# A three-branch decoder layer on one core: mLSTM, then cross-attention, then differential attention, with the output projection in two parts

## The chip, the cores and the metric

The kernel runs on one core of one Trainium2 chip. The metric is device time in microseconds (us) of one execution; of several executions of one program the median is taken. TensorE (PE in the profile) multiplies matrices, VectorE (DVE), ScalarE (ACT) and GpSimd (POOL) work on vectors, and SyncE (SP) only issues transfers (DMA) between device memory (DRAM) and the core's own memory. Each engine runs its instructions in the order in which they stand.

## What is computed

The layer normalises x (1024 tokens x 1024), projects it by one matrix of 9 groups of 512 columns, lets three groups of four heads work on the result, gates each, and maps the 1536 columns back onto the residual stream. All is float32.

```
h = rmsnorm(x, norm_g)
x_m, o_m, z_m, q_d, k_d, v_d, z_d, q_c, z_c = split(h @ w_in)         # 9 x 512
# mLSTM: q, k of silu(conv(x_m)), v of x_m; gates of (q, k, v); 8 chunks of 128 tokens,
# each with the state C, n of the chunk before it
y_m = (head_layernorm(sigmoid(o_m) * mlstm(q, k, v, gates)) + skip * x_cv) * silu(z_m)
# differential attention: two causal softmax maps a head (64 wide each), one less lam times the other
y_d = rmsnorm((softmax(q0 k0) - lam * softmax(q1 k1)) @ v_d) * silu(z_d)
# cross-attention on 256 rows of mem
y_c = softmax(q_c k_m) @ v_m * silu(z_c)
out = rmsnorm(x + concat(y_m, y_d, y_c) @ w_out, final_g)
```

## The kernel before

**Tiles.** Tokens lie in 8 row blocks of 128. Each large product is made of operands that are split in a high and a low part, so that a product over 128 rows of the inner dimension is three matmuls (high-high, high-low, low-high); a projection of 128 columns for 512 tokens is 8 x 3 = 24 matmuls of 128x512. `load_w` loads a weight block of 512 KB ahead of its use, in the order in which `plan_w` lists them, and splits it on POOL and DVE.

**What sets the order.** The code is written in one order, and a scheduler then places each engine's instructions in a fixed order of its own, so that work of several stages stands mixed. Buffers come from pools (`BUFS`): 16 "h" buffers hold the normalised and transposed x (`hT`), 8 "w" the split weights, 12 "qk", 5 "g" (halves, for gates), 4 "vd", 4 "p", 2 "pT", 2 "od"; a tile waits until the one that had its buffer is done. In PSUM, where matmuls write, there are two buffers each of three kinds.

**The order in the code.** (1) The norm and transposes of mem, `km_head`, the eight `x_block`, `vm_cols`, the cross heads (`cross_weights`, `cross_proj`, `cross_core`). (2) `vd_cols`, then four heads of differential attention: `diff_proj(h)` makes q and k; `diff_block(h, j)` treats the 128 queries of row block j against (j+1) blocks of 128 keys: scores of two maps (`ds`, L417, L418, L420), a row maximum on DVE (L421), exponentials on ACT (L424), a scaling on POOL (L428), the difference on DVE (L430), transposes on PE (`dpt`, L437), copies on ACT and DVE (L441, L439), the product with v (`dov`, L444) and its copy (L445). The j of a head run 0, 7, 1, 6, 2, 5, 3, 4. `diff_z` makes the gate, `diff_finish` norms and stores a head's rows to the DRAM tensor Yd. (3) The mLSTM: `xm_proj`, `om_cols`, `kv_block`, `qk_head`, gates, and then `chunk(c)` and `chunk_out(c)`. (4) The output: `load_wo` loads w_out (12 transfers of 512 KB), `out_prefetch(c)` reads rows back from Yd, and `out_block(c)` multiplies all 12 blocks of 128 columns by w_out, adds x, norms and stores.

Stages 3 and 4 are interleaved: the gate product `zm` (`zm_half`) stands among the first chunks, and out_block(c) stands beside chunk(c+2) and chunk_out(c+1). A chunk reads back from DRAM what stage 3 wrote there: k and v (`kvc`), q and k (`t`), a row of gate numbers broadcast to all 128 partitions (`rbc`, twice 256 KB), and, in chunk_out, two gates (`soz`) and the skip term (`skc`): 2.25 MB a chunk.

The loop that mixes the last two stages:

```
    for c in range(NB):
        if 0 < c and c + 2 < NB:
            chunk(c + 2)
        if 0 < c < NB - 1:
            chunk_out(c + 1)
        if 1 < c + 1 < NB:
            out_prefetch(c + 1)
        out_block(c)
```

Of the kernel before, what the change touches and what calls it, by code (L numbers as in the profile page):

```python
# [32 lines left out]
def hybrid_layer(ctx: ExitStack, tc: tile.TileContext, x, mem, norm_g, w_in, conv_w, conv_b, wq_m, wk_m,  # L33
# [76 lines left out]
    for cg in range(2):  # L110
        plan_w(w_in, C_VD + 256 * cg, f"wvd{cg}", True)
    for h in range(H):
        for c0, n_, hh in ((C_QD, "wqd", h), (C_KD, "wkd", h), (C_ZD, "wzd", h - 1)):
            if hh >= 0:
                plan_w(w_in, c0 + hh * P, f"{n_}{hh}")
    plan_w(w_in, C_OM, "wom0", True)
    plan_w(w_in, C_ZD + 3 * P, "wzd3")
    for h in range(H):
        plan_w(w_in, C_XM + h * P, f"wxm{h}")
    plan_w(w_in, C_OM + 256, "wom1", True)  # L120
    for h in range(H):
# [49 lines left out]
    def norm_transpose(src, blocks, g_, tag, sink):  # L171
        gbc, gsrc = g_
        for b in blocks:
# [16 lines left out]
    mT = [[slot("vd", f"mT{g}{part}", F32R).rearrange("p (k m) -> p k m", k=4) for part in range(2)]  # L190
          for g in range(2)]
# [142 lines left out]
    split_w(vmh, vml, vm, pool)
    mn = cst.tile([P, H], F32, name="mn")
    sk = cst.tile([P, H], F32, name="sk")
    cb = cst.tile([P, H], F32, name="cb")
    cw = cst.tile([P, 4, H], F32, name="cw")
    bif = cst.tile([P, 8], F32, name="bif")
    load(out=mn, in_=mnorm_g[0].rearrange("(h p) -> p h", p=P))  # L340
    load(out=sk, in_=skip_m[0].rearrange("(h p) -> p h", p=P))
    load(out=cb, in_=conv_b[0].rearrange("(h p) -> p h", p=P))
    for k in range(4):
        load(out=cw[:, k, :], in_=conv_w[0][k].rearrange("(h p) -> p h", p=P))
# [549 lines left out]
```

## Time and profile before

| | us |
|---|---|
| median of 3 runs | 817.94 (817.21 to 820.07) |
| the profiled execution | 819.47 |
| its span, from the first instruction to the last | 817.7 |
| TensorE busy | 770.1 |

The page has a line for each engine with its busy time, and the span in slices; the same table can be had for stretches that one chooses, with the clock that TensorE was granted (1.00 is 2.4 GHz, 0.50 is 1.2 GHz) and the share of time in which the 16 DMA engines were busy. In the order of time the span holds: the start and the cross heads (0 to 240 us), differential attention with products of the mLSTM among it (240 to 545), the rest of the mLSTM's preparation (545 to 605), the chunks with the output projection (605 to 745), and the rest of the output projection. Lists of waits say for how long an engine stood idle ahead of a kind of instruction, and which instruction released it; the timeline gives single instructions with the idle time before them in brackets.

### The profile page before, as it was taken

Reading aid. Unit: us, or ns where it says so; the run is one execution under the profiler, and the core shown is the slowest. Engines: PE = TensorE matmul, PEld = TensorE weight load, DVE = VectorE, ACT = ScalarE, POOL = GpSimd, SP = SyncE. Lnnn points to the kernel's source line nnn. Section 1 sums busy time; section 2 is a strip of 40 time slices with the busy share of each in tenths; the row PEclk is TensorE's granted clock in tenths of the full one; section 3 lists DMA queues with packets and bytes.
Section 4 is the critical chain, followed back from the end, with each engine's and each line's share of the span. In section 5 each row is a group of like instructions: output and inputs, shape, how many; then the busy total and the mean of one; then the engine's idle time right before and its main releaser. Section 6 shows DMA issues by size and latency. Waiting matters only on the chain.

```text
span 817.7 us, 11784 instructions
## 1 busy us (share of the span) xinstructions
PE 770.1 (94%) x4432; PEld 663.9 (81%) x4432; DVE 445.2 (54%) x922; ACT 322.3 (39%) x753; POOL 192.6 (24%) x248
## 2 busy tenths in 40 slices
PE   4999999999999999989999999999786879989996
PEld 3988888899988888878898888998565768777886
DVE  5785244342257667667724578533633597556532
ACT  3435234331134455545554437544472342222211
POOL 5443113121111122313103312412132332212000
PEclk9999999999999999999999999999898999999999
DMA  9920312122110001100122020245897997763001
GB/s 254 316 83 15 89 53 78 31 61 78 52 52 27 26 28 51 52 26 25 54 72 71 27 78 26 61 172 181 258 314 205 299 270 248 220 185 115 26 26 52
DMA packets 106416, 89.09 MB, mean 109 GB/s; under 512 B 10480, under 2 KB 91376, under 8 KB 106360
## 3 DMA queue, kind: packets, MB, share of 16 engines
q1 hardware_dynamic: 106216, 88.08, 35.7%
q8 instruction: 35, 0.57, 0.3%
q10 hardware_dynamic: 144, 0.26, 0.1%
q14 instruction: 21, 0.17, 0.1%
HBM read 65.23 MB, written 23.10 MB: 108 GB/s over the span
## 4 chain that ended last, share of the span: by engine, by line
PE 76%; DMA 11%; DVE 4%; issue 3%; POOL 2%; SPq 2%; ACT 2%; POOLq 0%; DVEq 0%; ACTq 0%
PE op L806 8%; PE om L158 6%; PE zd L149 5%; PE kd L149 5%; PE xm L149 5%; PE qd L149 5%; DMA rbc<-RBd 5%; PE qc L149 5%; PE zc L149 5%; PE vd L158 5%; PE zm L149 4%; PE dov L444 4%; PE ds L417 2%; PE ds L418 2%; PE dpt L437 2%
## 5 line engine op out<-in xcount | busy, mean ns | idle before, releaser
L806 PE MATMUL op<-wo,yh 128*128 128x512 f32 (+1 forms) x272 | 84.1, 391 | 2.4 <-DVE szm L667 2.4
L424 ACT ACTIVATE dp<-ds,dnb 128x128 f32<-128x128 f32 (+7 forms) x64 | 47.2, 740 | 55.3 <-DVE dnb L422 52.2
L149 PE MATMUL zm<-hT,wzm 128*128 128x512 f32 x192 | 51.0, 421 | 11.0 <-DVE szm L667 8.1
L806 PEld LDWEIGHTS op<-wo,yh 128*128 128x128 f32 x272 | 50.6, 193 | 12.5 <-DVE szm L667 2.8
L428 POOL TENSOR_SCALAR dp<-dp,dsum 128x128 f32<-128x128 f32 (+7 forms) x32 | 27.0, 844 | 135.8 <-DVE dsum L427 90.6
L421 DVE TENSOR_REDUCE dnb<-ds 128x1 f32<-128x128 f32 (+7 forms) x64 | 47.3, 752 | 19.9 <-PE ds L420 19.7
L149 PEld LDWEIGHTS zm<-hT,wzm 128*128 128x128 f32 x192 | 38.6, 205 | 20.4 <-DVE szm L667 8.7
L806 PE MATMUL op<-wo,yl 128*128 128x512 f32 (+1 forms) x136 | 52.6, 387 | 0.0
L158 PE MATMUL om<-wom,hT 128*128 128x256 f32 x384 | 52.4, 287 | 0.0
L149 PE MATMUL kd<-hT,wkd 128*128 128x512 f32 x192 | 49.6, 402 | 0.0
L149 PE MATMUL xm<-hT,wxm 128*128 128x512 f32 x192 | 48.7, 400 | 0.0
L149 PE MATMUL zd<-hT,wzd 128*128 128x512 f32 x192 | 48.7, 400 | 0.0
L149 PE MATMUL qd<-hT,wqd 128*128 128x512 f32 x192 | 48.3, 399 | 0.0
L806 PE MATMUL op<-wo,ymr 128*128 128x512 f32 (+1 forms) x204 | 47.8, 382 | 0.1
L158 PEld LDWEIGHTS om<-wom,hT 128*128 128x128 f32 x384 | 47.4, 189 | 0.1
L149 PE MATMUL qc<-hT,wqc 128*128 128x512 f32 x192 | 47.2, 394 | 0.0
L149 PE MATMUL zc<-hT,wzc 128*128 128x512 f32 x192 | 46.8, 393 | 0.0
L158 PE MATMUL vd<-wvd,hT 128*128 128x256 f32 x384 | 46.2, 279 | 0.0
L158 PEld LDWEIGHTS vd<-wvd,hT 128*128 128x128 f32 x384 | 45.1, 188 | 0.3
L806 PEld LDWEIGHTS op<-wo,ymr 128*128 128x128 f32 x204 | 36.5, 188 | 8.2 <-DVE ymr L84 0.5
L149 PEld LDWEIGHTS qc<-hT,wqc 128*128 128x128 f32 x192 | 35.5, 188 | 7.3
L149 PEld LDWEIGHTS zc<-hT,wzc 128*128 128x128 f32 x192 | 35.5, 188 | 7.3
(331 smaller groups left out, 1658.3 us busy)
## 6 DMA issues: line engine op xcount, KB each, us to landing
wor<-in_w_out_dram SPq DMA_DIRECT2D x12, 512.0 KB, 6.1
xx<-in_x_dram SPq DMA_DIRECT2D x8, 512.0 KB, 5.8
KVd<-kv SPq DMA_DIRECT2D x8, 512.0 KB, 2.7
QKd<-qkt SPq DMA_DIRECT2D x16, 256.0 KB, 3.6
kvc<-KVd SPq DMA_DIRECT2D x16, 256.0 KB, 7.1
yr<-Yd SPq DMA_DIRECT2D x8, 512.0 KB, 10.0
t<-QKd SPq DMA_DIRECT2D x8, 512.0 KB, 7.1
rbc<-RBd SPq DMA_DIRECT2D x16, 256.0 KB, 9.6
```

Of the source, the lines that this page charges most:

```text
L149: pe.matmul(acc, lhsT=w[wp][:, k, :], rhs=hT_ap(t, k, hp, 0, 512), start=n == 0, stop=n == 23)
L158: pe.matmul(acc, lhsT=hT_ap(b // 4, k, hp, (b % 4) * P, P), rhs=w2[k // 4][wp][:, k % 4, :], start=n == 0, stop=n == 23)
L417: pe.matmul(sc[:, c0:c0 + w_], lhsT=lhs, rhs=KA[h][m][:, c0:c0 + w_], start=True, stop=False)
L418: pe.matmul(sc[:, c0:c0 + w_], lhsT=lhs, rhs=KB[h][m][:, c0:c0 + w_], start=False, stop=not last)
L421: dve.tensor_reduce(out=nb[:, m:m + 1], in_=sc[:, :n], op=ALU.max, axis=AX.X)
L424: act.activation(p_[:, :n], sc[:, :n], AF.Exp, scale=0.125, bias=nb[:, m:m + 1], accum_out=sums[:, m:m + 1])
L428: pool.tensor_scalar(out=pp[1][:, :n], in0=pp[1][:, :n], scalar1=sums[:, 1:2], scalar2=0.0, op0=ALU.mult, op1=ALU.add)
L437: pe.transpose(out=pt[:, i * P:(i + 1) * P], in_=pp[0][:, (g + i) * P:(g + i + 1) * P], identity=ident)
L444: pe.matmul(acc, lhsT=pT[:, i * P:(i + 1) * P], rhs=vd[h][:, i, :], start=i == 0, stop=i == j)
L806: pe.matmul(accs[nh][:, c0:c0 + n_], lhsT=yp[a_], rhs=wo[kp, nh, b_][:, o:o + n_], start=k == 2 * KORD[0] and n == 0, stop=k == 2 * KORD[- ...
```

## The change

The arithmetic is the same but for the order of sums. The order of the stages is turned round:

- The start: pairs of `x_block`, and after each pair `xm_pair(h, g)` for the four heads, that is xm for 256 tokens by matmuls of 256 columns (384 in all in place of 192 of 512). 6 of the 8 normed rows come from "qk" buffers, and the low parts of wxm0 and wxm1 are made on POOL.
- The mLSTM's preparation follows (conv, kv_block, qk_head, gates, both om_cols), then the chunks, with `zm_head`, the norm of mem, `km_head`, `vm_cols` and `vd_cols` among them. chunk_out no longer splits its rows for the output projection, but stores them to Yd (8 stores of 256 KB), which has 12 column blocks now: 0 to 3 mLSTM, 4 to 7 cross, 8 to 11 differential.
- Then the cross heads, then the four heads of differential attention. Loads of w_out stand after head 2: into "h" buffers, which the last uses of hT have let go, and for two of six pairs of blocks into "w" buffers.
- The output projection is cut in two. `out_part(c)` multiplies the mLSTM and cross columns (48 matmuls a row block) and adds x; `out_final(c)` multiplies the differential columns (24), adds, norms and stores. out_part's rows (`yr`) take an "od" buffer. The order is out_part(0) to (3), diff_finish(3), out_part(4) to (7), out_final(0) to (7). The last row block's two halves are scaled by DVE one after the other; before, ACT and DVE did one half each.

```diff
-    for h in range(H):
-        for i, j in enumerate((0, 7, 1, 6, 2, 5, 3, 4)):
-            diff_block(h, j)
-            if h and i == 2:
-                diff_finish(h - 1)
-        if h + 1 < H:
-            diff_proj(h + 1)
-        diff_z(h)
-        if h == 2:
-            om_cols(0)
...
-        ymr = ymr_[c] = slot("pT", f"ymr{c}", F32R)
-        split(ymr[:, :512], ymr[:, 512:], ym)
+        store(out=Y[c][:, 0:4, :].rearrange("p k s -> p (k s)"), in_=ym)
...
+    def out_part(c):
+        xr = XR[c] = slot("qk", f"xr{c}")
+        load(out=xr, in_=x[c * P:(c + 1) * P, :])
+        yr = slot("od", f"yr{c}")
+        load(out=yr, in_=Y[c][:, 0:8, :].rearrange("p k s -> p (k s)"))
+        yp = [slot("qk", f"yp{c}{i}", F32R) for i in range(2)]
+        split(yp[0], yp[1], yr)
         for nh in range(2):
+            acc = pj(f"oa{c}{nh}")
+            products(acc, yp, (0, 1, 4, 5), nh)
             cs = slice(nh * 512, (nh + 1) * 512)
             dve.tensor_tensor(out=xr[:, cs], in0=acc, in1=xr[:, cs], op=ALU.add)
...
+    for g in range(4):
+        x_block(2 * g)
+        x_block(2 * g + 1)
+        for h in range(H):
+            xm_pair(h, g)
...
+    om_cols(0)
+    om_cols(1)
     chunk(0)
     chunk(1)
+    for h in range(H):
+        zm_head(h)
...
     chunk_out(0)
...
     chunk(2)
+    km_head(0)
+    km_head(1)
     chunk_out(1)
+    km_head(2)
+    chunk(3)
+    km_head(3)
+    chunk_out(2)
+    vm_cols(0)
+    chunk(4)
+    vm_cols(1)
...
+    diff_proj(0)
+    for h in range(H):
+        for i, j in enumerate((0, 7, 1, 6, 2, 5, 3, 4)):
+            diff_block(h, j)
+            if h and i == 2:
+                diff_finish(h - 1)
+        if h < H - 1:
+            diff_proj(h + 1)
+        if h < H - 2:
+            diff_z(h)
+        if h == H - 2:
+            for kps, t in (((0, 1), 0), ((4, 5), 1)):
+                diff_z(h, (t,))
+                diff_z(h + 1, (t,))
+                for kp in kps:
+                    load_wo(kp, "w", "h")
+    for kp in (2, 3):
+        load_wo(kp, "p", "w")
+    for c in range(4):
+        out_part(c)
+    diff_finish(H - 1)
+    FG.append(slot("p", "fg"))
+    load(out=FG[0], in_=final_g.partition_broadcast(P))
+    for c in range(4, NB):
+        out_part(c)
     for c in range(NB):
+        out_final(c)
```

Three places of the order that the scheduler made follow; a name such as ds361 is the scores of head 3, row block 6, map 1, and the number behind the underscore is that of a buffer.

TensorE in head 3 of differential attention, before: the scores of (3,6), then what stands behind them (xm01 is xm of head 0).

```order
L417 MATMUL ds361_4316<-KA31_3774,QA31_3708 128x512
L418 MATMUL ds361_4316<-KB31_3776,QA31_3708 128x512
L417 MATMUL ds361_4316<-KA31_3774,QA31_3708 128x384
L418 MATMUL ds361_4316<-KB31_3776,QA31_3708 128x384
L420 LDWEIGHTS identb_75
L420 MATMUL ds361_4316<-maskb_77,identb_75 128x128
L149 MATMUL xm01_4642<-hT110_99,wxm00_4612 128x512
L444 MATMUL dov37_4233<-vd3_1648,dpT37_4220 128x128 x8
L437 MATMUL dpt310_4268<-ident_70,dp310_4253 128x128 x2
L149 MATMUL xm01_4642<-hT111_100,wxm00_4612 128x512
```

TensorE at the same place, after:

```order
L348 MATMUL ds361_6528<-KA31_6126,QA31_6060 128x512
L349 MATMUL ds361_6528<-KB31_6128,QA31_6060 128x512
L348 MATMUL ds361_6528<-KA31_6126,QA31_6060 128x384
L349 MATMUL ds361_6528<-KB31_6128,QA31_6060 128x384
L351 LDWEIGHTS identb_75
L351 MATMUL ds361_6528<-maskb_77,identb_75 128x128
L368 MATMUL dpt370_6433<-ident_70,dp370_6416 128x128 x4
L368 MATMUL dpt374_6439<-ident_70,dp370_6416 128x128 x4
L375 MATMUL dov37_6445<-vd3_2821,dpT37_6432 128x128 x8
L348 MATMUL ds320_6567<-KA30_6125,QA30_6059 128x384
L349 MATMUL ds320_6567<-KB30_6127,QA30_6059 128x384
```

Between the scores of (3,6) and the next ones there stood products of xm; now only the differential attention's own transposes and products with vd stand there. So it is for nine blocks in a row, from (2,3) to (3,3), which have 40 of the 144 key blocks of the four heads.

TensorE where the output projection begins, after (oa is out_part's sum; wo00 is w_out's first pair of blocks):

```order
L348 MATMUL ds331_6657<-KA31_6126,QA31_6060 128x512
L349 MATMUL ds331_6657<-KB31_6128,QA31_6060 128x512
L351 LDWEIGHTS identb_75
L351 MATMUL ds331_6657<-maskb_77,identb_75 128x128
L707 MATMUL oa00_6761<-wo000_6267,yp00_6757 128x512
L707 MATMUL oa00_6761<-wo001_6268,yp00_6757 128x512
L707 MATMUL oa01_6787<-wo010_6273,yp00_6757 128x512
L707 MATMUL oa01_6787<-wo011_6274,yp00_6757 128x512
L375 MATMUL dov32_6593<-vd3_2821,dpT32_6587 128x128 x3
L707 MATMUL oa00_6761<-wo000_6267,yp01_6758 128x512
```

The first of out_part's 384 matmuls stands behind the scores of (3,3), the last block but one of head 3.

SyncE's queue at the first chunks, before (wor is a raw block of w_out, SZd a store of a gate, QKd one of q and k):

```order
L778 DMA wor50_5975<-in_w_out_dram 128x2x512
L668 DMA SZd0_4597<-szm30_5764 128x4x128
L554 DMA QKd_4594<-qkt31_5248 128x4x128
L668 DMA SZd1_4598<-szm01_5858 128x4x128
L688 DMA t10_5544<-QKd_4594 128x1024
L691 DMA rbc0_5546<-RBd_4599 128x4x128 x2
L684 DMA kvc1_5590<-KVd_4596 128x512
L685 DMA kvc1_5590<-KVd_4596 128x4x128
L688 DMA t11_5594<-QKd_4594 128x1024
L691 DMA rbc1_5596<-RBd_4599 128x4x128 x2
L744 DMA soz0_5770<-SOd0_2235 128x512
L745 DMA soz0_5770<-SZd0_4597 128x512
```

SyncE's queue at the same place, after:

```order
L488 DMA QKd_122<-qkt30_1216 128x4x128
L488 DMA QKd_122<-qkt31_1229 128x4x128
L606 DMA t10_1753<-QKd_122 128x1024
L609 DMA rbc0_1755<-RBd_127 128x4x128 x2
L602 DMA kvc1_1799<-KVd_124 128x512
L603 DMA kvc1_1799<-KVd_124 128x4x128
L488 DMA QKd_122<-qkt31_1229 128x4x128
L606 DMA t11_1803<-QKd_122 128x1024
L609 DMA rbc1_1805<-RBd_127 128x4x128 x2
L589 DMA SZd0_125<-szm00_1886 128x4x128
```

The loads of w_out that stood among those of the first chunks are gone from there, and so are the reads of Yd behind them; the chunks' own loads are the same.

## Rows read from the trace of the kernel before

**Rows 1.** Page: busy us of TensorE, share of span, instructions.

```profile
PE 770.1 (94%) x4432; PEld 663.9 (81%) x4432; DVE 445.2 (54%) x922; ACT 322.3 (39%) x753; POOL 192.6 (24%) x248
```

**Rows 2.** Stages: start:end, length, busy us per engine, PEclk, DMA share, GB/s.

```profile
0.00:60.00 60.00, 46.44 (x294) 42.56 (x295) 41.70 (x64) 23.15 (x53) 28.42 (x31) 1.00 0.77 223
...
240.00:545.00 305.00, 302.76 (x1841) 262.95 (x1840) 189.70 (x385) 154.93 (x366) 71.15 (x92) 0.99 0.17 51
545.00:605.00 60.00, 52.46 (x258) 42.13 (x256) 30.30 (x41) 32.16 (x58) 14.66 (x11) 0.94 0.73 227
605.00:680.00 75.00, 61.19 (x309) 50.34 (x310) 43.25 (x117) 26.80 (x56) 25.57 (x37) 0.93 0.94 273
680.00:745.00 65.00, 60.84 (x311) 50.66 (x310) 42.77 (x126) 13.51 (x33) 13.72 (x23) 0.97 0.61 191
```

**Rows 3.** PE waits, 545 to 745: us in total, times, longest.

```profile
PE zm L149 <- DVE szm L667: 8.1, 2, 5.7
```

**Rows 4.** Timeline: start us, us, instruction [idle before <-releaser].

```profile
622.96 0.69 DVE L705 TENSOR_TENSOR rbc<-t,rbc 128x512 f32<-128x512 f32 x1 [2.52 <-DMA rbc<-RBd]
...
624.30 2.07 PE L149 MATMUL zm<-hT,wzm 128*128 128x512 f32 x4 [5.72 <-DVE szm L667]
```

**Rows 5.** Chain that ended last: start us, us, engine, tile, line, count.

```profile
605.74 5.55 PE zm L149 x23
...
624.30 5.66 PE zm L149 x16
```

**Rows 6.** DMA issues: tiles, queue, count, KB each, median us to landing.

```profile
rbc<-RBd SPq DMA_DIRECT2D x16, 256.0 KB, 9.6
...
wqd1r<-in_w_in_dram SPq DMA_DIRECT2D x1, 512.0 KB, 3.6
```

**Rows 7.** Groups by line, DVE, 240 to 545: busy us, mean ns | idle.

```profile
L421 DVE TENSOR_REDUCE dnb<-ds 128x1 f32<-128x128 f32 (+7 forms) x64 | 47.3, 752 | 19.9 <-PE ds L420 19.7
...
L430 DVE SCALAR_TENSOR_TENSOR dp<-dp,dsum,dp 128x128 f32<-128x128 f32 (+7 forms) x32 | 27.4, 855 | 13.1 <-POOL dp L428 12.7
...
L445 DVE COPY od<-dov 128x128 f32<-128x128 f32 x32 | 9.2, 289 | 22.5 <-PE dov L444 22.2
L422 DVE TENSOR_SCALAR dnb<-dnb 128x1 f32<-128x1 f32 x64 | 9.0, 149 | 0.9
...
L439 DVE COPY dpT<-dpt 128x512 f32<-128x512 f32 (+3 forms) x16 | 7.8, 489 | 5.9 <-PE dpt L437 5.6
```

**Rows 8.** Same view, PE: the product with vd.

```profile
L444 PE MATMUL dov<-vd,dpT 128*128 128x128 f32 x288 | 40.5, 282 | 0.0
```

**Rows 9.** Timeline, PE, head 3 blocks with other products between.

```profile
503.49 0.61 PE L444 MATMUL dov<-vd,dpT 128*128 128x128 f32 x4
503.93 0.60 PE L437 MATMUL dpt<-ident,dp 128*128 128x128 f32 x4
504.29 6.43 PE L149 MATMUL xm<-hT,wxm 128*128 128x512 f32 x27
```

**Rows 10.** Timeline, PE, end of head 1, nothing between.

```profile
356.61 0.48 PE L417 MATMUL ds<-KA,QA 128*128 128x512 f32 x1
...
357.40 0.89 PE L444 MATMUL dov<-vd,dpT 128*128 128x128 f32 x6
...
361.40 0.33 PE L417 MATMUL ds<-KA,QA 128*128 128x128 f32 x1 [1.49 <-ACT dp L424]
...
361.85 2.93 PE L444 MATMUL dov<-vd,dpT 128*128 128x128 f32 x12
...
365.26 2.08 PE L149 MATMUL kd<-hT,wkd 128*128 128x512 f32 x8
```

**Rows 11.** Groups by shape: xm by 512 columns, vd by 256.

```profile
L149 PE MATMUL xm<-hT,wxm 128*128 128x512 f32 x192 | 48.7, 400 | 0.0
...
L158 PE MATMUL vd<-wvd,hT 128*128 128x256 f32 x384 | 46.2, 279 | 0.0
```

**Rows 12.** Same view, DVE: the last step of the output rows.

```profile
L842 DVE SCALAR_TENSOR_TENSOR xr<-xr,frstd,fg 128x512 f32<-128x512 f32 x14 | 9.9, 747 | 1.4 <-POOL frstd L80 1.4
```

More of the change, by code (lines that the diff above doesn't have):

```diff
@@ L188, in norm_transpose @@
                 split(dhi, dlo, pt[:, k0 * P:(k0 + kk) * P].rearrange("p (k t) -> p k t", k=kk))
[L190 to L191 removed]
+    gbc = slot("od", "gbc")
     hT = {}
@@ L334, in hybrid_layer @@
[L334 to L344, printed above, removed]
@@ new lines, in hybrid_layer, with load_wo @@
+    wov = w_out.rearrange("(k p) c -> p k c", p=P)
+    XR, FG = {}, []
+    def load_wo(kp, rtag, tag):
+        for nh in range(2):
+            raw = slot(rtag, f"wor{kp}{nh}")
+            load(out=raw.rearrange("p (k c) -> p k c", k=2), in_=wov[:, 2 * kp:2 * kp + 2, nh * 512:(nh + 1) * 512])
+            hi, lo = wo[kp, nh] = [slot(tag, f"wo{kp}{nh}{part}", F32R) for part in range(2)]
+            act.activation(hi, raw, AF.Copy)
+            (pool if nh else dve).tensor_tensor(out=lo, in0=raw, in1=hi.bitcast(F32), op=ALU.subtract)
@@ new lines, in hybrid_layer @@
+    cb = cst.tile([P, H], F32, name="cb")
+    cw = cst.tile([P, 4, H], F32, name="cw")
+    bif = cst.tile([P, 8], F32, name="bif")
+    load(out=mn, in_=mnorm_g[0].rearrange("(h p) -> p h", p=P))
+    load(out=sk, in_=skip_m[0].rearrange("(h p) -> p h", p=P))
+    load(out=cb, in_=conv_b[0].rearrange("(h p) -> p h", p=P))
+    for k in range(4):
+        load(out=cw[:, k, :], in_=conv_w[0][k].rearrange("(h p) -> p h", p=P))
+    load(out=bif, in_=b_if[0].partition_broadcast(P))
+    dnc = cst.tile([P, H], F32, name="dnc")
@@ new lines, in hybrid_layer @@
+    load(out=dnc, in_=dnorm_g[0].rearrange("(h p) -> p h", p=P))
+    dve.tensor_scalar(out=dnc, in0=dnc, scalar1=1.0 - LAM_INIT, scalar2=None, op0=ALU.mult)
+    lamt = slot("p", "lamt")
+    lamv = lamt[:, :256].rearrange("p (i e) -> p i e", i=4)
+    for i, v in enumerate((lam_q1, lam_k1, lam_q2, lam_k2)):
+        load(out=lamv[:, i, :], in_=v[0].partition_broadcast(P))
+    nlam = cst.tile([P, 1], F32, name="nlam")
+    lt = lamt[:, 256:384].rearrange("p (i e) -> p i e", i=2)
+    ls = cst.tile([P, 2], F32, name="ls")
@@ new lines, in hybrid_layer @@
+    for i in range(2):
+        dve.tensor_tensor(out=lt[:, i, :], in0=lamv[:, 2 * i, :], in1=lamv[:, 2 * i + 1, :], op=ALU.mult)
+    dve.tensor_reduce(out=ls, in_=lt, op=ALU.add, axis=AX.X)
+    act.activation(ls, ls, AF.Exp)
+    dve.tensor_tensor(out=nlam, in0=ls[:, 1:2], in1=ls[:, 0:1], op=ALU.subtract)
+    dve.tensor_scalar(out=nlam, in0=nlam, scalar1=LAM_INIT, scalar2=None, op0=ALU.subtract)
+    gate_weights()
+    mlstm_weights()
+    for h in range(H):
+        conv(h)
+    for b in range(NB):
+        kv_block(b)
@@ new lines, in hybrid_layer @@
+    chunk(3)
[4 more added lines that the diff above has]
+    vm_cols(1)
+    vmh = slot("qk", "vmh", F32R).rearrange("p (b c) -> p b c", b=2)
+    vml = slot("qk", "vml", F32R).rearrange("p (b c) -> p b c", b=2)
+    split_w(vmh, vml, vm, pool)
+    chunk_out(3)
+    chunk(5)
+    vd = [slot("vd", f"vd{h}").rearrange("p (b c) -> p b c", b=NB) for h in range(H)]
+    vd_cols(0)
+    chunk_out(4)
+    chunk(6)
+    vd_cols(1)
+    chunk_out(5)
+    chunk(7)
+    chunk_out(6)
```

270 lines of the change are left out of this document (93 added, 177 removed).

## The prediction

> **What bounds the kernel now.** I read the page's engine line first: TensorE is busy 770.1 of 817.7 us, so what can be won is in the 47.6 us in which it idles, and in the time in which it works at the lower clock [rows 1]. Then the table of stages, for where that is. The reader is to see three things in it. From 240 to 545, differential attention, TensorE idles for 2.2 us in 305. In the first 60 us it idles for 13.6. From 545 to 745, the end of the mLSTM's preparation and the chunks, it idles for 7.5 + 13.8 + 4.2 = 25.5 us, and there alone the mean granted clock is below 1.00 (0.94, 0.93, 0.97) while the DMA engines are busy 0.61 to 0.94 of the time at 191 to 273 GB/s [rows 2]. Then the waits in that stretch: the longest kind is zm waiting for DVE's szm, 8.1 us in two waits [rows 3]. The timeline says why: DVE stood 2.52 us for a transfer of rbc and could only then do the szm that frees PSUM; TensorE had by then stood for 5.72 us [rows 4]. So the releaser is DVE by name and a transfer by cause. The chain of waits shows the second price: 16 zm matmuls took 5.66 us after that wait, where 23 took 5.55 a little earlier [rows 5]; that is 1.8 us lost at 1.2 GHz behind one wait. If TensorE were busy all through, the clock columns would make 60 x 0.06 + 75 x 0.07 + 65 x 0.03 = 10.8 us; part of the low clock falls in idle time, and I take 6.5. So the stretch loses 25.5 + 6.5 = 32 us, for want of transfers: rbc takes 9.6 us to land, while a weight block of twice its size takes 3.6 in a quiet stage [rows 6].
>
> **The change, part by part.**
>
> *The chunks without the output projection's transfers.* w_out's 6 MB, the reads of Yd and x (4 MB each) and the result's stores leave the chunks, and zm, km, vm and vd stand beside these. By my count of the code the stretch from om to the last chunk now transfers 43.5 MB beside some 220 us of matmuls, 198 GB/s, against the 273 at which the chunks' stretch before stands with its DMA engines 0.94 busy [rows 2]. What is late next: the first chunk's reads, which still stand in SyncE's queue behind the last stores of q and k; DVE, which still stands in order for rbc ahead of szm; and each chunk's own chain over DVE, ACT and POOL. I leave 13 us of the 32 there: 2 in conv and kv, 3 at the first chunk, 6 in the others, 2 of low clock. **Gain 19.** Bounds: 6 (only zm's 8.1 us less one wait is won) and 30.
>
> *Head 3 without other products.* This is the price of the turn. By the order, nine blocks with 40 of 144 key blocks have no other product between them. Before, up to 27 xm matmuls, 6.43 us, stood between two steps of a block [rows 9]. TensorE's own work in these nine: a map's scores against 5 key blocks start at 356.61 and end at 357.40, 0.79 us [rows 10], so 0.32 a key block for two maps; 4 passes with v take 0.44 us and 4 transposes 0.36 [rows 9], and the trace has two passes with v and one transpose for a key block (288 passes for the 144 [rows 8]). That is 0.32 + 0.22 + 0.09 = 0.63, and 40 x 0.63 = 25 us. DVE's work is in five groups: 47.3 + 27.4 + 9.2 + 9.0 + 7.8 = 100.7 us for the 144 [rows 7], so 28 us for 40, and DVE is needed twice within each block. So the stretch lasts at least 28 us, a loss of 3, were DVE never to wait. The only place of the trace that looks like it is the end of head 1: from 356.61 to 365.26 nothing stands between; 8.65 us for two maps' scores (0.79 and 0.45), 18 passes with v (2.0) and ten transposes at the 0.09 above (0.9), 4.1 us in all [rows 10]. TensorE waited there and then worked at the lower clock: 12 passes with v took 2.93 us, 0.24 each against 0.11. At that rate the 25 us take 53, a loss of 28. But DVE did other work there too (the split of a weight and of q), which head 3 has not. The blocks share two score buffers, so a block can't start its scores until the exponentials of the one before are done. I take **18**, between 3 and 28 and nearer to the row of head 1, since it alone shows a stretch without other work.
>
> The Trainium skill says of this kind of stretch (TensorE: Matmul & The Clock Gate, section "A second HAM failure mode: psum-queue depth-cycling") that a kernel whose TensorE idles shortly between groups of matmuls has its clock swing between its levels and loses throughput by it. By that rule the whole of the 25 us would run at 1.2 GHz, an estimate of 50 us and a loss of 25 in place of my 18. The trace agrees at the end of head 1 (0.24 us a pass, just after a wait of 1.49 us); it is the first rival.
>
> *Other parts.* xm in 256 columns: vd has 384 such in 46.2 us, 0.241 a pair, and 27 xm matmuls of 512 took 6.43, 0.238 each [rows 9, 11]; 192 pairs cost **0.5** more. The first 60 us: the idle 13.6 [rows 2] stays, since x's first block must be loaded and normed as mem's was; xm for a pair of row blocks can start only when both are transposed, at four places, 1 us each, and what km covered before is not there: **2** (-2 to 5). The output: 384 + 192 matmuls of 512 columns and 24 of 256 are the same work as before; out_final has half of DVE's pieces for a third of the matmuls, and the last block's two halves run one after the other at 0.75 us each [rows 12], where two engines did them side by side: **2** (0 to 4). What leaves and comes besides (mLSTM rows through Yd, 2 MB stored and read) lies beside matmuls in stretches in which the DMA engines are 0.17 busy [rows 2]; out of them it would cost a landing or two, some 5 us. Heads 0 to 2 and the cross heads keep what stood between their blocks: nothing.
>
> *Sum.* -19 + 18 + 0.5 + 2 + 2 = +3.5 us. The profiled execution took 819.47 us, its span and 1.8 around it; that is 1.5 above the median of 817.94 and inside the runs' spread. On the profiled time the sum is 823.0, on the median **821.4**, 0.4% slower.
>
> **The rivals.** All times are from the median.
>
> *The clock stays low in head 3.* Place: the nine blocks; price: 28 in place of 18, with the gain at 13 since the chunks' own chain, not the transfers, then sets their pace. -13 + 28 + 4.5 = +19.5, so 837. For it: the end of head 1. Against: DVE has less to do beside. It decides where the clock is at 0.50 for most of the stretch.
>
> *The mLSTM gives back nearly all, and the kernel is faster.* Place: the chunks; price: 30 of the 32 us. -30 + 18 + 4.5 = -7.5, so 810. For it: the waits there begin at transfers [rows 4], and those are what the change thins out. Against: DVE still waits for rbc in order. It decides from a gain of 25 on, or from a loss in head 3 under 12 at the gain of 19.
>
> *The two cancel.* A gain of 22 or a loss in head 3 of 15: within 2.5 us of 817.9.
>
> **How the numbers follow.** A measurement of this kernel can tell about 0.3%, 2.5 us: from 815.5 to 820.4 is "the same". My forecast, 820.4 to 830, has 0.36; the low clock, 830 to 845, 0.15; the faster kernel, 800 to 815.5, 0.32; the two cancelling, 0.17. So faster 0.32, same 0.17, slower 0.51, and the likeliest is 821.4. The range must reach into the cases on either side: the faster one's 810 less 3, 807, and the low clock's 837, which leave about 0.1 on each side.
>
> **What would show each step.** Right: in the stage of the chunks TensorE's idle time and low clock together about 13 us, rbc landing in clearly under 9.6; in head 3 a stretch with TensorE busy some 0.6 of the time, DVE most of it, and a granted clock under 1.00; the last matmul of the differential heads followed by out_part without a gap. Wrong: if the chunks idle as before, the gain is not there, and what waits there is a chain of engines; if head 3 runs with TensorE over 0.8 busy at full clock, my 18 is too much. A gap ahead of out_part's first product, which needs an "od" buffer, a load and a split, would be a cost that the sum lacks.

## The result

The changed kernel takes 868.64 us (median of 4 runs, 867.62 to 870.14), the kernel before beside it 818.74 (817.21 to 820.07). The ratio is 1.061, 95% interval 1.0585 to 1.0638: slower by 50 us, where 821.4 was predicted and 807 to 837 was the range. The way was right, the size was not: the likeliest sum was +3.5 us.

### The profile page after: what moved, and what is told of

The parts are those of the page before. It is cut to its first block, busy times and chain, and to the rows that moved or that the text cites. A ratio compares the mean times of both kernels' runs of the same rounds, so it can differ in the third digit from the quotient of the medians.

```text
span 866.2 us, 12198 instructions
## 1 busy us (share of the span) xinstructions
PE 789.4 (91%) x4600; PEld 683.8 (79%) x4600; DVE 455.6 (53%) x936; ACT 319.8 (37%) x752; POOL 186.1 (21%) x248
## 2 busy tenths in 40 slices
DMA packets 108721, 93.30 MB, mean 108 GB/s; under 512 B 10736, under 2 KB 91632, under 8 KB 108664
## 4 chain that ended last, share of the span: by engine, by line
PE 57%; DMA 7%; DVE 5%; POOL 2%; ACT 1%; issue 1%; DVEq 0%; POOLq 0%; SPq 0%; ACTq 0%
PE oa L707 10%; PE kd L150 5%; PE qd L150 5%; PE qc L150 5%; PE zc L150 5%; PE ob L707 5%; PE zd L150 4%; DMA rbc<-RBd 4%; PE dov L375 3%; PE vd L159 3%; PE ds L348 2%; PE ds L349 1%; DMA wvm10r<-in_w_mem_kv_dram 1%; DMA wvd01r<-in_w_in_dram 1%; PE sc L275 1%; PE oc L297 1%
## 5 line engine op out<-in xcount | busy, mean ns | idle before, releaser
L707 PE MATMUL oa<-wo,yp 128*128 128x512 f32 x384 | 91.0, 396 | 0.0
L707 PEld LDWEIGHTS oa<-wo,yp 128*128 128x128 f32 x384 | 71.5, 188 | 16.2
L159 PE MATMUL vd<-wvd,hT 128*128 128x256 f32 x384 | 53.0, 299 | 4.6 <-DVE vd L412 4.1
L460 PE MATMUL xm<-hT,wxm 128*128 128x256 f32 x384 | 51.8, 300 | 5.3 <-DVE hT L84 3.3
L460 PEld LDWEIGHTS xm<-hT,wxm 128*128 128x128 f32 x384 | 50.5, 205 | 7.0 <-DVE hT L84 3.6
L159 PEld LDWEIGHTS vd<-wvd,hT 128*128 128x128 f32 x384 | 50.4, 203 | 5.6 <-DVE vd L412 4.5
L375 PE MATMUL dov<-vd,dpT 128*128 128x128 f32 x288 | 41.2, 286 | 4.0 <-DVE szd L404 2.1
L707 PE MATMUL ob<-wo,ydp 128*128 128x512 f32 (+1 forms) x204 | 44.7, 379 | 0.0
L375 PEld LDWEIGHTS dov<-vd,dpT 128*128 128x128 f32 x288 | 38.1, 197 | 7.6 <-DVE szd L404 2.7
L707 PEld LDWEIGHTS ob<-wo,ydp 128*128 128x128 f32 x204 | 36.5, 188 | 8.3 <-ACT ob L738 1.2
```

Of the source, the lines that this page charges most:

```text
L159: pe.matmul(acc, lhsT=hT_ap(b // 4, k, hp, (b % 4) * P, P), rhs=w2[k // 4][wp][:, k % 4, :], start=n == 0, stop=n == 23)
L375: pe.matmul(acc, lhsT=pT[:, i * P:(i + 1) * P], rhs=vd[h][:, i, :], start=i == 0, stop=i == j)
L460: pe.matmul(acc, lhsT=wxm[h][wp][:, k, :], rhs=hT_ap(t, k, hp, c0, 256), start=n == 0, stop=n == 23)
L707: pe.matmul(acc, lhsT=yk[a_], rhs=wo[kp, nh][b_][:, k * 512 + c0:k * 512 + c0 + n_], start=n == 0, stop=n == last)
```

## The profile after, and where the 50 us went

The span is 866.2 us, 48.5 longer. The stages of the changed kernel, in the columns of [rows 2]: 0 to 60 is the start, 150 to 360 the chunks with what stands beside them, 677 to 717.3 the blocks of head 3 that have no other product between them, and from 840 on it is the end.

```profile
0.00:60.00 60.00, 40.25 (x267) 38.00 (x268) 24.16 (x50) 20.61 (x45) 17.46 (x22) 0.89 0.54 148
150.00:180.00 30.00, 27.02 (x140) 22.99 (x139) 6.62 (x12) 12.81 (x26) 4.79 (x11) 0.94 0.83 204
180.00:360.00 180.00, 143.48 (x970) 132.44 (x969) 92.12 (x259) 35.92 (x99) 45.89 (x67) 0.91 0.57 163
600.00:677.00 77.00, 74.74 (x410) 61.63 (x409) 51.67 (x103) 40.50 (x94) 20.96 (x23) 1.00 0.20 66
677.00:717.30 40.30, 32.89 (x208) 25.87 (x207) 32.29 (x84) 24.35 (x68) 14.91 (x20) 0.96 0.18 54
840.00:866.20 26.20, 18.84 (x94) 15.69 (x92) 13.28 (x27) 6.50 (x19) 2.19 (x4) 0.96 0.26 100
```

I count as lost in a stretch TensorE's idle time and one minus the mean granted clock, times the stretch; that is an upper measure, since low clock in idle time is counted twice. The start loses 19.8 + 6.6 = 26.4 us against 13.6 before. The chunks lose 3.0 + 36.5 of idle time and 18 of clock, 57.5, against 25.5 + 10.8 = 36.3 in [rows 2]. Head 3's bare stretch loses 7.4 + 1.6 = 9.0 and the 77 us ahead of it 2.3, together 11.3; the kernel before loses 2.2 + 3.1 = 5.3 in all of differential attention (240 to 545 in [rows 2]). The end is alike. So, against before, the start costs some 13 us, the chunks 21 and head 3 with what lies ahead of it 6: 40 of the 48.5. Where the other 8 lie this count doesn't show.

What TensorE waits for in the chunks' stage (in all, times, longest), and, below it, what DVE waits for; L617 and L623 are the two steps that read the two halves of rbc:

```profile
PE pn L634 <- DVE rbc L623: 12.0, 3, 7.7
PE pn L634 <- DVE wc L643: 5.8, 1, 5.8
PE pS L615 <- DMA t<-QKd: 4.8, 2, 3.0
```

```profile
DVE rbc L617 <- DMA rbc<-RBd: 36.5, 8, 8.4
DVE rbc L623 <- DMA rbc<-RBd: 20.0, 8, 3.4
```

DVE stood 56.5 us for rbc. The same two rows of the kernel before, 545 to 745 us, come to 38.4:

```profile
DVE rbc L699 <- DMA rbc<-RBd: 21.8, 6, 7.6
DVE rbc L705 <- DMA rbc<-RBd: 16.6, 8, 3.6
```

The timeline of one chunk, 303 to 325 us, shows the loop. SyncE stores the rows of an earlier chunk, and only then issues the two reads of rbc; DVE gets the first half at 312.7 and the second at 316.8, 11 us after the issue; TensorE's pn has by then waited 7.70 us; and the steps on DVE that follow release the next store, behind which the next reads of rbc stand.

```profile
303.23 0.33 SPq L685 DMA_DIRECT2D Yd<-t  x1
...
305.36 0.92 SPq L609 DMA_DIRECT2D rbc<-RBd  x2
...
312.71 0.87 DVE L617 TENSOR_SCALAR rbc<-rbc,colA 128x128 f32<-128x128 f32 x4 [6.63 <-DMA rbc<-RBd]
...
316.80 0.69 DVE L623 TENSOR_TENSOR rbc<-t,rbc 128x512 f32<-128x512 f32 x1 [3.21 <-DMA rbc<-RBd]
...
317.55 0.80 PE L634 MATMUL pn<-wc,rbc 128*128 128x129 f32 x2 [7.70 <-DVE rbc L623]
...
321.84 0.32 SPq L685 DMA_DIRECT2D Yd<-t  x1
...
324.40 0.92 SPq L609 DMA_DIRECT2D rbc<-RBd  x2
```

The line of all reads of rbc, after (issue time min/median/max in ns, first and last start in us), says what it adds up to: 8 chunks from 171.7 to 324.8, 153 us.

```profile
L609 SPq DMA_DIRECT2D rbc<-RBd x16: 370/492/1805, 171.7 to 324.8; - x16
```

At the start, the order in which ACT and DVE stand is to be seen: ACT norms the third pair of row blocks (L181) only behind its copies of xm (L463), which wait for TensorE, so the transposes wait 3.95 us; then DVE stands 2.94 us for the loads of lam (L775) ahead of the split of x, and xm waits 3.31.

```profile
36.23 0.60 ACT L463 ACTIVATE xm<-xm 128x512 f32<-128x512 f32 x1 [0.84 <-PE xm L460]
36.72 1.05 ACT L181 ACTIVATE xn<-xx 128x1024 f32<-128x1024 f32 x1
...
40.14 1.06 PE L187 MATMUL xpt<-ident,xn 128*128 128x128 f32 x8 [3.95 <-DVE rs_x L79]
...
46.60 0.22 DVE L775 TENSOR_TENSOR lamt<-lamt 128x64 f32<-128x64 f32 x1 [2.94 <-DMA lamt<-in_lam_k_dram]
...
48.96 1.44 PE L460 MATMUL xm<-hT,wxm 128*128 128x256 f32 x5 [3.31 <-DVE hT L84]
```

## The experiments

Four theories were set against each other for the chunks: A, the reads stand behind stores in SyncE's queue; B, they lack buffers; T, transfers as such; and that rbc's own landing sets the chunk's loop. The expectations name more, each where it is needed. In two runs the start and w_out's splits were tested. "Both edits" below are the new start and km and vm outside the "qk" buffers.

### Queue, buffers, start

**e1_actq**: the store of the mLSTM rows on ACT's queue.

```diff
-        store(out=Y[c][:, 0:4, :].rearrange("p k s -> p (k s)"), in_=ym)
+        nc.scalar.dma_start(out=Y[c][:, 0:4, :].rearrange("p k s -> p (k s)"), in_=ym)
```

> The changed kernel (868.6) with one edit: chunk_out issues its store of mLSTM rows on ACT's queue, not SyncE's. Theory A (queue): between 240 and 345 us the next chunk's reads stand on SyncE behind that store, which waits for DVE, 24.8 us in three kinds of waits; then the reads leave earlier and the time falls by 15 to 30, to 839 to 854. Theory B (buffers): the reads need a buffer of the 12 'qk' that the stored rows still hold, so it matters little where the store is issued: 863 to 869. Theory C (the chunk's own chain: 11 us for rbc, then some 8 on the engines): 866 to 870.

863.18 us (861.45 to 863.66): 5.5 less. The row on which theory A rested, SyncE waiting for DVE ahead of that store in the changed kernel, was this:

```profile
SPq L685 <- DVE mrs L673: 24.8, 3, 8.9
```

These are three waits of one kind; the 24.8 us of a queue's waiting were worth 5.5.

**e2_qk**: km and vm out of the "qk" buffers.

```diff
-    kmh = slot("qk", "kmh", F32R).rearrange("p (h m) -> p h m", h=H)
-    kml = slot("qk", "kml", F32R).rearrange("p (h m) -> p h m", h=H)
-    vm = slot("qk", "vm").rearrange("p (b c) -> p b c", b=2)
+    kmh = slot("p", "kmh", F32R).rearrange("p (h m) -> p h m", h=H)
+    kml = slot("p", "kml", F32R).rearrange("p (h m) -> p h m", h=H)
+    vm = slot("pT", "vm").rearrange("p (b c) -> p b c", b=2)
```

> The changed kernel with another edit alone: the cross branch's km (high and low part) in 'p' buffers and vm in a 'pT' buffer, so that three of the 12 'qk' buffers come free for the chunks in the middle of the stage. Theory B (buffers): the reads of chunks 3 and 4 leave earlier, the time falls by 15 or more, to below 854. Theory A (queue): the stores still hold SyncE, 860 to 868. Theory C: 866 to 870.

849.18 (845.29 to 849.81): 19.5 less. **e3_both** has this and the edit of e1.

> The changed kernel with both edits, the store on ACT's queue and km, vm out of the 'qk' buffers. If queue and buffers each hold the reads, more than the better of the two alone: 830 to 845. If only one does, within 3 us of that one. Theory C: 864 to 870.

853.65 (849.17 to 855.42): no better than buffers alone, rather 4 us worse, which I can't explain. So, by these runs, the queue costs something only while buffers are scarce.

**e4_start**: x normed a pair of row blocks ahead, lam's sums moved to just ahead of differential attention.

```diff
-    for g in range(4):
-        x_block(2 * g)
-        x_block(2 * g + 1)
-        for h in range(H):
-            xm_pair(h, g)
+    for b in range(4):
+        x_block(b)
+    for g in range(4):
+        for h in range(H):
+            xm_pair(h, g)
+        for b in (2 * g + 4, 2 * g + 5):
+            if b < NB:
+                x_block(b)
...
```

> The changed kernel with only its start rearranged: four row blocks of x normed ahead of the first xm and each later pair one step ahead of the xm that covers it, and the small sums for lam moved to just before differential attention. Theory S: of the 20 us that TensorE idles in the first 60 (13.6 before the change) and the 0.89 clock, some 10 us come from the order of ACT and DVE (norms behind xm's copies, the split of x behind lam's loads): 856 to 861. Rival: the first transposes wait for transfers, and what is won is lost when the chunks begin: 866 to 870.

848.91 (848.24 to 849.75): 19.7 less, more than expected. The stage table of this run shows 7.2 us more of TensorE's work in the first 60 and a clock of 1.00 there; that is 14 us. The other 6 came from the chunks, which begin at another moment: by the count above they lose 29.2 + 16.2 = 45 us from 150 to 330, not 57.5.

```profile
0.00:60.00 60.00, 47.43 (x362) 45.84 (x363) 32.24 (x58) 26.66 (x56) 17.02 (x23) 1.00 0.57 155
150.00:330.00 180.00, 150.77 (x969) 137.88 (x967) 95.83 (x262) 40.72 (x106) 46.68 (x72) 0.91 0.67 179
```

### Both edits, and what does not help further

**e5_start_qk** has both edits.

> The changed kernel with the rearranged start and with km and vm out of the 'qk' buffers. If the two losses are separate, their gains add: 868.6 - 19.7 - 19.4 = 829.5 (827 to 833). Rival: both only shift when the chunks begin against the transfers, and the sum is less: 838 to 849.

839.71 (837.89 to 841.86): 29 less than the changed kernel, not 39. The two gains overlap, as the rival had it, and the stage of the chunks still idles for 24 us of 180, at a clock of 0.93:

```profile
150.00:330.00 180.00, 155.78 (x1030) 142.68 (x1029) 93.49 (x265) 40.89 (x109) 47.72 (x73) 0.93 0.60 181
```

Four runs tried to take that away. **e6_om** writes om behind the first two chunks.

> The kernel with both edits, and om (384 matmuls, some 46 us) written behind the first two chunks in place of ahead of them. Theory F (want of other products): the chunks have a pace of their own, some 18 us each, set by transfers and DVE, and TensorE idles there for some 25 us only because too few other products stand beside them; then om beside the first chunks takes 8 to 18 us off, 812 to 822. Rival T (transfers): the chunks' reads then compete with the stores of q, k, v and the gates and come later by as much: 827 to 835.

839.95 (837.70 to 840.52). It says nothing on theory F: the scheduler left om's matmuls in the same places as in e5_start_qk, and the whole order of TensorE, DVE, ACT and POOL with them. As a repeat it shows that 0.2 us is chance. **e8_cross** writes the projections of cross head 0 ahead of vd, and there they did move, by 73 us (257 instead of 331 for the first).

```diff
+    cross_weights(0)
+    cross_proj(0, 0)
+    cross_proj(0, 1)
     vd_cols(0)
     chunk_out(4)
```

> The kernel with both edits, and the projections of cross head 0 (96 matmuls, 22.6 us) written beside the later chunks, ahead of vd, its gate in 'g' buffers as for all cross heads. Theory F: 6 to 15 us less than with both edits alone, 815 to 824. Rival T, or 'qk' buffers scarce again: within 3 us of it or slower.

841.73 (837.19 to 846.16): no gain. From 150 to 330 us TensorE is busy for 156.6 us, in e5_start_qk for 155.8, so a want of products is not it. **e9_pool** puts the steps that wait for rbc on POOL, **e10_ldq** the chunk's reads on ACT's queue.

```diff
-            dve.tensor_scalar(out=hs(t3, h), in0=hs(rbc, h), scalar1=colA[:, c, h:h + 1], scalar2=None, op0=ALU.add)
+            pool.tensor_scalar(out=hs(t3, h), in0=hs(rbc, h), scalar1=colA[:, c, h:h + 1], scalar2=0.0, op0=ALU.add, op1=ALU.add)
...
-        dve.tensor_tensor(out=t2[:, 512:], in0=t1[:, :512], in1=t2[:, 512:], op=ALU.mult)
+        pool.tensor_tensor(out=t2[:, 512:], in0=t1[:, :512], in1=t2[:, 512:], op=ALU.mult)
```

> The kernel with both edits (839.7), and the two steps of a chunk that wait for rbc (adding colA, and the product of q with rbc's second half) on POOL in place of DVE. Theory D: the chunks' remaining loss, 24 us of TensorE idle from 150 to 330, is DVE standing in order for rbc (36.5 + 20.0 us in the changed kernel) ahead of the szm, vd and km steps that TensorE needs; then 8 to 20 us less, 820 to 832. Rival L: the chunk itself is late (t and rbc land late, TensorE's own pS and pn wait), and POOL's slower steps lengthen it: 838 to 846.

> The kernel with both edits, and the five reads of a chunk (k, v, q with k, rbc twice) issued on ACT's queue, so that they stand behind none of SyncE's stores and weight loads. Theory A again, now that buffers are free: 5 to 15 us less, 825 to 835. Theory D or plain lack of transfer rate: within 3 us of 839.7.

839.49 (838.29 to 840.26) and 839.30 (837.70 to 841.34): neither gains anything. From 150 to 330 us TensorE is busy for 156.2 and 155.9 us, in e5_start_qk for 155.8. So the queue from which rbc is read doesn't count once buffers are free. On the engine that stands for rbc the run says less: POOL takes 2.8 and 1.26 us for a chunk's two steps, DVE 0.88 and 0.69, and these 2.5 us more a chunk may have taken back what DVE won. **e7_wo** tested head 3: w_out's low parts all on POOL (`pool` for `(pool if nh else dve)` in load_wo).

> The kernel with both edits, and all low parts of w_out made on POOL, where DVE made half of them (2.6 and 2.9 us each time on the chain in head 3). If DVE bounds the stretch of head 3 that has no other products, 2 to 5 us less than without this edit; if the blocks' own chain or the score buffers do, within 1.5 us of it.

835.85 (834.55 to 838.96): 3.9 less, as expected if DVE bounds that stretch. From 640 to 700 us TensorE is busy for 55.3 us at 1.00, in e5_start_qk for 52.5 at 0.97, and TensorE's wait of 2.1 us for DVE's szd in that stretch is gone (first row e5_start_qk, second e7_wo):

```profile
640.00:700.00 60.00, 52.52 (x314) 42.26 (x314) 46.84 (x112) 36.36 (x95) 19.34 (x23) 0.97 0.22 69
```

```profile
640.00:700.00 60.00, 55.34 (x344) 45.46 (x343) 47.56 (x113) 37.78 (x95) 22.84 (x25) 1.00 0.31 102
```

**e12_poolwo** joins it with e9.

> The kernel with both edits, the rbc steps on POOL, and w_out's low parts on POOL (this last alone gave 835.9). If the two are independent, the change by the rbc steps alone less 4 us; under theory D 816 to 828.

837.75 (837.17 to 839.00): 1.7 less than e9_pool, where 4 were expected, and not better than w_out's parts alone. So the 3.9 of e7_wo may be partly chance.

### Leaving transfers out

**e13_nowload** leaves out the 12 loads of weights for km, vm and vd, **e14_nowor** the 12 loads of w_out in the kernel before (`raw = fg` for the slot and its load).

> The kernel with both edits (839.7), in which the weights of km, vm and vd (12 loads, 6 MB) are not loaded: the splits read a tile of hT in their place, so those three projections are of other numbers. Theory T (transfers): the reads of the chunks then share the DMA engines with less, and the stage loses 10 to 20 us less: 820 to 830. Theory L (the chunk's own chain): within 4 us of 839.7.

> The kernel before, with w_out's 12 loads (6 MB) left out of the stage of the chunks: final_g's tile stands in for its values. It tests the prediction's gain alone. If the 32 us that TensorE loses there come from the output projection's transfers, 8 to 20 us less than before, 798 to 810. If they come from the chunk's own chain, within 4 us of before.

841.39 (836.10 to 842.00) against 839.71, and 817.98 (815.29 to 819.00) against 817.74 for the kernel before beside it, ratio 0.9994 (0.9972 to 1.0016). Six MB fewer in the stage, on either side, change nothing. The rows for the stage (e13, 150 to 330; e14, 545 to 745, and the kernel before below it) show the transfers thinner, 147 GB/s and 202 where e5_start_qk has 181 and the kernel before 233, and TensorE no better off:

```profile
150.00:330.00 180.00, 155.83 (x1023) 143.02 (x1022) 94.10 (x265) 40.88 (x109) 48.00 (x73) 0.91 0.56 147
```

```profile
545.00:745.00 200.00, 178.10 (x882) 146.52 (x881) 119.86 (x284) 72.09 (x149) 54.62 (x72) 0.93 0.67 202
```

```profile
545.00:745.00 200.00, 174.49 (x876) 143.13 (x875) 116.33 (x282) 72.47 (x146) 53.95 (x70) 0.95 0.77 233
```

Nor does a half of rbc land earlier with the thinner traffic: 9.8 us in e13 (9.1 in e5_start_qk), 9.4 in e14 (9.6 before, [rows 6]).

```profile
rbc<-RBd SPq DMA_DIRECT2D x16, 256.0 KB, 9.8
```

```profile
rbc<-RBd SPq DMA_DIRECT2D x16, 256.0 KB, 9.4
```

**e15_norbc** leaves out the reads of rbc:

```diff
-        for g in range(2):
-            load(out=rbc[:, g * 512:(g + 1) * 512].rearrange("p (h s) -> p h s", h=H),
-                 in_=RBd[g, :, tok].partition_broadcast(P))
...
-            dve.tensor_scalar(out=hs(t3, h), in0=hs(rbc, h), scalar1=colA[:, c, h:h + 1], scalar2=None, op0=ALU.add)
+            dve.tensor_scalar(out=hs(t3, h), in0=hs(t1, h), scalar1=colA[:, c, h:h + 1], scalar2=None, op0=ALU.add)
...
-        dve.tensor_tensor(out=t2[:, 512:], in0=t1[:, :512], in1=t2[:, 512:], op=ALU.mult)
+        dve.tensor_tensor(out=t2[:, 512:], in0=t1[:, :512], in1=t1[:, 512:], op=ALU.mult)
```

> The kernel with both edits, in which rbc is not read (16 reads, 4 MB): the two steps use the chunk's q and k in its place, so the chunks' decay factors are of other numbers. If rbc's late landing is the wait that counts, 10 to 25 us less than 839.7: 815 to 830. If any other read of the chunk takes its place, within 5 us.

810.49 (807.18 to 813.35): 29 less than e5_start_qk. The stage idles for 3.0 us and the clock is 1.00:

```profile
150.00:330.00 180.00, 177.03 (x1200) 161.94 (x1199) 112.64 (x306) 50.05 (x132) 59.20 (x81) 1.00 0.54 172
```

Four MB of this one read are worth 29 us, where 6 MB of others were worth none. **e16_bpool** puts the steps for rbc on POOL in the kernel before.

> The kernel before, with the two steps that wait for rbc on POOL in place of DVE. If DVE's wait ahead of szm costs there what the prediction took it for (the longest TensorE wait, 5.7 us, and 1.8 of low clock behind it), 5 to 12 us less than before: 806 to 813. If the wait only moves, within 3 us of before.

822.68 (819.94 to 824.57), ratio 1.006 (1.004 to 1.008): slower. TensorE's waits of zm for szm fall from 8.1 us [rows 3] to 2.4, but those of mt, a step of chunk_out, rise from 2.7 to 10.1, and DVE waits 21.0 us for POOL's mrs ahead of mt:

```profile
PE mt L762 <- DVE t L758: 10.1, 4, 4.2
...
PE zm L149 <- DVE szm L667: 2.4, 1, 2.4
```

So the wait that the prediction named moved and nothing was won. This doesn't show that it cost nothing, since the steps take 2.5 us a chunk longer on POOL here too.

### rbc in pieces of 4 KB

The gate numbers lie in DRAM as two rows of 1024 tokens for each of 4 heads, so a chunk's read brings each partition eight pieces of 512 bytes in two reads. Laid out by chunk, it is one read and one piece of 4 KB, of the same bytes to the same partitions (the store of those rows changes with it):

```diff
-    RBd = dr.tile([2, H, S], F32, name="RBd")
+    RBd = dr.tile([NB, 2, H, P], F32, name="RBd")
...
-        store(out=RBd[0], in_=rows(rd))
-        store(out=RBd[1], in_=rows(rint))
+        for g, src in enumerate((rd, rint)):
+            store(out=RBd[:, g].rearrange("b h s -> h b s"), in_=chk(src))
...
-        for g in range(2):
-            load(out=rbc[:, g * 512:(g + 1) * 512].rearrange("p (h s) -> p h s", h=H),
-                 in_=RBd[g, :, tok].partition_broadcast(P))
+        load(out=rbc, in_=RBd[c].rearrange("g h s -> (g h s)").partition_broadcast(P))
```

**e17_rb4k** has it with both edits and e7's.

> The kernel with both edits and w_out's low parts on POOL (835.9), in which the two rows of gate numbers lie in DRAM by chunk, so that one read brings both halves of rbc to each partition in one piece of 4 KB, where two reads did it in eight pieces of 512 bytes. If the pieces are what is slow, most of the 29 us that leaving rbc out gave: 808 to 822. If it is the broadcast of one source to 128 partitions, within 4 us of 835.9.

805.89 (803.20 to 806.54), ratio to the kernel before 0.9855 (0.9821 to 0.9888); 30 less than the 835.85 without it. The stage is as without rbc at all, at the same DMA share as in e5_start_qk (0.59 and 0.60); DVE's wait for rbc is 9.9 us in all; the reads leave within 102 us, where it was 129 in e7_wo and 153 in the changed kernel:

```profile
150.00:330.00 180.00, 177.48 (x1203) 162.39 (x1202) 111.09 (x306) 50.49 (x132) 60.19 (x81) 1.00 0.59 195
```

```profile
DVE rbc L615 <- DMA rbc<-RBd: 9.9, 5, 6.4
```

```profile
L608 SPq DMA_DIRECT2D rbc<-RBd x8: 320/406/1297, 158.0 to 260.0; - x8
```

**e18_brb4k** has it alone on the kernel before.

> The kernel before with the same layout of the gate numbers. If the pieces are slow, and rbc is what TensorE's 32 us there hang on: 793 to 808. If the broadcast is: within 3 us of before. If rbc is not the bottleneck there: the same, although rbc lands in clearly less than 9.6 us.

802.56 (799.95 to 805.20), ratio 0.9831 (0.9793 to 0.9869). This beats both kernels. From 605 to 680 TensorE is busy for 71.5 us where [rows 2] has 61.2, and the transfers move 326 GB/s at a share of 0.92 where it was 273 at 0.94; DVE waits 13.4 us for rbc, not 38.4. A whole rbc of 512 KB lands in 7.1 us, where each half took 9.6 [rows 6]. Other reads land earlier with it, those of Yd for the output (`yr`) in 5.4 us and not 10.0; but they did so in e14_nowor too (4.5), where nothing was won. The gain doesn't come from another order of work: at least 4,404 of TensorE's 4,432 matmuls and 869 of DVE's 922 instructions stand in the order of the kernel before, by the names of their tiles. The lines of e18_brb4k, and behind them `yr` before:

```profile
605.00:680.00 75.00, 71.54 (x377) 60.01 (x378) 55.81 (x150) 29.96 (x62) 30.17 (x39) 0.98 0.92 326
```

```profile
DVE rbc L697 <- DMA rbc<-RBd: 13.4, 4, 6.2
```

```profile
yr<-Yd SPq DMA_DIRECT2D x8, 512.0 KB, 5.4
...
rbc<-RBd SPq DMA_DIRECT2D x8, 512.0 KB, 7.1
```

```profile
yr<-Yd SPq DMA_DIRECT2D x8, 512.0 KB, 10.0
```

**e19_arb4k** has it alone on the changed kernel.

> The changed kernel (868.6) with the gate numbers laid out by chunk, one read of 4 KB pieces for rbc, and nothing else. If rbc makes the whole loss of the chunks' stage, buffers included, the stage's loss of some 50 us shrinks to some 10 and the kernel takes 825 to 835: the start's 12 us and head 3's 10 remain. If the buffers cost by themselves, 836 to 850.

828.33 (827.03 to 829.70): 40 of the changed kernel's 50 us, though its "qk" buffers are as scarce as without it. The start's loss and head 3's are still in it. Against e18_brb4k the change itself, with rbc mended on both sides, still costs 26 us; with the start, the buffers and w_out's splits mended too (e17_rb4k) it costs 3, and their runs overlap (803.2 to 806.5 and 800.0 to 805.2).

## Why the prediction was wrong

**The gain of 19 in the chunks** is the step that failed. It read the waits rightly down to rbc [rows 4], and then took the cause to be the amount transferred: 273 GB/s at a share of 0.94, less of it after the change, so less waiting. e14_nowor takes the w_out part of that step alone, 6 MB out of the stage, and gives nothing; in the changed kernel all of it is out, the stage moves 163 GB/s at a share of 0.57 from 180 to 360 us, and loses more. What sets the pace there is how long a chunk waits for its rbc, over a loop of read, DVE, TensorE and the next read (e15_norbc, e17_rb4k, e18_brb4k). The change didn't shorten that loop. It lengthened it: from the first rbc read to the last the eight chunks take 153 us against 114 before. Cross tiles in the buffers that the reads need have the larger part in this (e2_qk: 129 us, 19.5 less in all), the store to DRAM that the next reads stand behind a small one (e1_actq: 152 us, 5.5 less in all). The change also put 79 us of km, vm and vd beside the chunks where the output's products had stood, whose part in it no run shows. The term came out as some +21, an error of 40. With rbc in one piece the changed kernel is 40 us faster (e19_arb4k), the kernel before 15 (e18_brb4k): the slow read costs 25 us more in the order that the change makes. The rows had the hint: rbc took 9.6 us for 256 KB while weights of 512 KB took 3.6 [rows 6]; the prediction put that down to traffic. One of its signs of being right even came, rbc landing in under 9.6 us:

```profile
rbc<-RBd SPq DMA_DIRECT2D x16, 256.0 KB, 7.3
```

But that is the median over single halves. A chunk needs both, and in the timeline above the second is there 11 us after the issue of the first.

**The rival "chunks' own chain"** was in the prediction as a reason for a smaller gain (13 in place of 19) and as a sign that the gain is not there, never as a loss. That a moved stage can run worse than before, since its buffers and its neighbours change, had no price in it, and the range ended at 837.

**Head 3 without other products**: +18 was forecast, the trace has 9.0 in the bare stretch and 11 with what lies ahead of it, 6 more than differential attention lost before. TensorE is busy for 0.82 of the bare stretch, which the prediction had as a sign that 18 is too much. The mechanism is there (DVE is busy 32.3 of 40.3 us; e7_wo, which relieves it, takes up to 3.9 off). The size was too much: at the end of head 1 [rows 10], on which the 18 leant, TensorE worked at the lower clock behind a wait of 1.49 us (0.24 us for a pass with v, against 0.11 in [rows 9]). In head 3 it did so once, behind a wait of 2.06 us (0.25 us for a pass), and from 690 to 710, with waits of up to 0.64 us, the granted clock is 1.00:

```profile
679.61 1.98 PE L375 MATMUL dov<-vd,dpT 128*128 128x128 f32 x8 [2.06 <-DVE szd L404]
```

```profile
310.00:320.00 10.00, 2.45 (x11) 2.45 (x12) 4.04 (x16) 0.80 (x2) 0.64 (x1) 0.73 0.72 132
...
680.00:690.00 10.00, 8.67 (x49) 6.85 (x49) 7.22 (x21) 6.63 (x18) 2.56 (x3) 0.84 0.26 80
690.00:700.00 10.00, 8.37 (x58) 6.51 (x56) 7.13 (x22) 5.36 (x16) 1.39 (x3) 1.00 0.00 0
700.00:710.00 10.00, 8.81 (x57) 7.02 (x58) 8.49 (x26) 6.64 (x23) 7.00 (x12) 1.00 0.01 2
```

By the Trainium skill (TensorE: Matmul & The Clock Gate, section "A second HAM failure mode: psum-queue depth-cycling") frequent short idling between groups of matmuls made one kernel's clock swing and cost it throughput. The trace agrees only in part: the mean granted clock in the bare stretch is 0.96, and it falls to 0.73 where TensorE had waited 7.70 us in the chunks (310 to 320 us). The prediction's 25 us by that rule, with the lower clock all through, went further than the section does, and further than the trace. The measurement decides.

**The start**: +2 was forecast with 5 as the upper bound; it is some 13. The step counted TensorE's boundaries and left out the order on ACT and DVE, which the order of the changed kernel would have shown: norms behind copies of xm, the split of x behind lam's loads. e4_start gives it back, and some more.

**xm in 256 columns, the output, the end**: +0.5 and +2 were forecast. The matmuls of xm are busy for 51.8 us on the page of the changed kernel and 48.7 before, part of it at the start's lower clock. The start, the chunks and head 3 leave some 8 of the 48.5 us; no run took these apart, so whether the two terms were right stays open.

**The rivals.** 837 for a low clock in head 3 came nearest in time, but its place was wrong. The faster kernel had 0.32 and was far off. That the kernel came out slower, to which the prediction gave 0.51, was luck: its +3.5 was a cost in head 3 put three times too high, less a gain that turned out a loss.

## What to carry to other kernels

A wait that ends with a transfer has two possible causes, the traffic around it or that transfer's own shape. Before one prices less traffic, one should leave out the traffic and, apart from it, the one transfer: here 6 MB gave 0 and 4 MB gave 29 us. And a stage that is moved must be priced as a new stage: what its reads stand behind, whose buffers it shares, and what stands beside it.

## What the runs showed of the hardware

One partition's 4 KB in eight pieces of 512 bytes and two reads, or in one piece and one read: the kernels differ by 15 us (before), 40 (changed) and 30 (mended), with the same bytes to the same 128 partitions. Whether the pieces, the second read or the layout in DRAM count more wasn't separated. The packets that the traces hold speak for the pieces. Of the packets of 512 bytes, 1,043 took over 100 ns before (the median is 27) and 842 in e14_nowor, but 110 in e18_brb4k and 117 where rbc isn't read at all (e15_norbc). The Trainium skill (DMA: Bandwidth & Descriptors, section "Specifications") sets 512 bytes as the least that a transfer needs for the full rate; by that the pieces of 512 would do. The traces disagree for this read: at a share of 0.92 to 0.94 the stage moved 273 GB/s with them and 326 without [rows 2]. Leaving out 12 loads of weights (e13_nowload), which took 8,384 packets off the program's 108,721, gave nothing, while the new layout took 7,239 off and gave 30 us (e17_rb4k). By the pages the main DMA queue took 35.7% of 817.7 us before, 33.0% of 817.2 in e14_nowor and 34.1% of 798.1 in e18_brb4k: 22 and 20 us less of the engines' time, for 0 and 15 us. So it is how late this read lands on a chunk's path that costs, not the DMA engines' time.
